# Moving the high and low activation parts of a split-precision trunk to fixed places modulo 512 bytes

## The chip, the cores and the metric

The kernel runs on one core of one Trainium2 chip. What counts is the device time of one launch in microseconds, from the first to the last instruction with a little around them. A time is a median over runs. A profile comes from one execution of its own.

The five engines have short names in the rows below: PE is TensorE (PEld its loading of weights), DVE is VectorE, ACT is ScalarE, POOL is GpSimd, and SP is the queue that issues the DMAs (SPq). SBUF is the on-chip memory, 128 partitions; an address here is always the byte address inside a partition.

## The reference

A decoder trunk of two layers on 256 tokens of width 1024, all in float32:

```python
h = half_step_swiglu(h, ...)            # FFN0:  h + 0.5 * ((silu(hn @ w_gate) * (hn @ w_up)) @ w_down)
h = h + hybrid_dsa_shortconv_mixer(...) # sparse attention next to a short gated convolution,
                                        # one input projection (2472 columns), one output projection
h = half_step_swiglu(h, ...)            # FFN1
h = half_step_swiglu(h, ...)            # FFN2
h = h + conformer_conv_module(...)      # pointwise + GLU, causal convolution of 31 taps, LayerNorm, pointwise
h = half_step_swiglu(h, ...)            # FFN3
return rms_norm(h, final_norm)
```

Each block normalises its input first (`hn` is the RMS norm of `h` times a gain). The inner width of the feed-forward blocks is 2816.

## The kernel before

**Split operands.** Each float32 operand of a projection is held as two parts: a high part, written by ScalarE in the type fp32r that TensorE reads, and a low part, the rest, written by VectorE. A product is three matmuls into the same PSUM tile, which the helper `mm3` issues (lines 254 to 256): weights high with activations high, weights high with activations low, weights low with activations high. In the trace these are `acc<-xh,whi`, `acc<-xl,whi` and `acc<-xh,wlo` (in the trace's names the moving operand comes first). The moving operand is 128 partitions by 256 tokens, 1,024 bytes in a partition; the weights are 128x128. `mm3a` (lines 259 to 261) does it with the activations as the loaded operand, for the first columns of the hybrid layer's input projection.

**Weights.** The class `Stream` brings all weights in tiles of up to 128x2048: a DMA on SP into `raw` (3 buffers), a copy on ScalarE into `whi` (5 buffers), a subtraction on VectorE into `wlo` (5 buffers). It runs ahead of TensorE by some tiles; the next load is issued when `wlo` has been formed. In the built program all of these tiles begin at 256 modulo 512.

**Activations.** `x` is the residual. `xh` and `xl` are its parts times the norm's gain, one tile for each that all blocks share, written by `x_split` (lines 276 to 281) as soon as a slice of `x` is final. Each tile is 128 floats longer than it has to be, and the table `X_AT` says for each norm at which float the part starts in it. In the feed-forward blocks `hh` and `hl` are the parts of the gated product, with places from the table `H_AT`. A feed-forward block has 11 groups of 256 gate and 256 up columns, 8 slices of the contraction each (gate and up), and then 8 output slices of 22 contraction slices (down). In the first group it stops at two places for the norm: `col_stats` (line 306, four matmuls of one column each, `tp<-ones,sqsum`) sums the squares, GpSimd raises the sum to a power (`rc`, line 313), and `row_of` (line 319, four small matmuls, `tp<-con,rc`) spreads the result over the tokens. All other matmuls of a block follow each other without another instruction of TensorE between them.

**Places before**, worked out from the tables and the built program, in bytes modulo 512, high and low:

| block | gate and up, or input projection | down, or output projection |
|---|---|---|
| FFN0 | 192, 192 | 192, 192 |
| hybrid layer | 192, 192 | convolution half (`yh`, `yl`) 192, 192; attention half (`cu`, `q4`) 160, 192 |
| FFN1 | 192, 448 | 192, 448 |
| FFN2 | 192, 64 | 192, 320 |
| conformer | 192, 192 | 128, 256 |
| FFN3 | 192, 320 | 192, 64 |

**The hybrid layer** takes its tiles from the pool `hyb`. `cu` holds the convolution's input (258 columns for each of 4 slices) and is later taken again for the high part of the attention's output; `q4` holds the transposed queries and is taken again for its low part (lines 703 and 704). `pv_out` and `o_lo` write these parts, `wo_part` (line 806) multiplies with them, first `yh` and `yl`, then the attention's. The order of its work is set by a planner, the class `Side`, from costs written out by hand.

Of the kernel before, what the change touches and what calls it, by code (L numbers as in the profile page):

```python
# [10 lines left out]
FT = mybir.dt.float32  # L11
FR = mybir.dt.float32r
# [6 lines left out]
S = 256  # L19
KT = 8  # L20
# [10 lines left out]
RAW_BUFS = 3  # L31
AHEAD = 3

X_AT = ((16, 16), (16, 16), (16, 80), (16, 112), (16, 16), (16, 48))
H_AT = ((112, 112), (112, 48), (112, 16), (112, 80))
DVE_CT = 2
LO_H = (2, 2, 1, 1, 1, 1, 1, 0)

# [150 lines left out]
def trunk_kernel(ctx: ExitStack, tc: tile.TileContext, xT, wgu, wdn, wza, wzq, wcv, wout, wp1, wp2,  # L189
# [33 lines left out]

    x = keep.tile([128, KT, S], FT, name="x")
    x_all = [keep.tile([128, KT * S + 128], FR, name=n) for n in ("xh", "xl")]
    xparts = [[t[:, o:o + KT * S].rearrange("p (k t) -> p k t", k=KT) for t, o in zip(x_all, at)] for at in X_AT]
    par = keep.tile([128, NP], FT, name="par")
    con = keep.tile([128, NC_], FT, name="con")
    ones = keep.tile([128, 128], FT, name="ones")
# [16 lines left out]
    def acc():  # L246
        return psum.tile([128, 512], FT, name="acc", bufs=6)
# [22 lines left out]
    norm = {}  # L270
# [3 lines left out]
        norm["parts"] = []  # L274

    def x_split(d):
        xh, xl = xparts[norm["g"]]
        g = par[:, P_G + norm["g"] * 8 + d:P_G + norm["g"] * 8 + d + 1]
        nc.scalar.activation(xh[:, d], x[:, d], AF.Copy, scale=g)  # L279
        nc.vector.scalar_tensor_tensor(xl[:, d], x[:, d], g, xh[:, d].bitcast(FT),  # L280
                                       op0=OP.mult, op1=OP.subtract)
# [14 lines left out]
    def x_ready(d):  # L296
        x_split(d)
        x_square(d)
# [29 lines left out]

    def ffn(f, gnext, last=False):
        with tc.tile_pool(name=f"ffn{f}", bufs=1, reuse_waits="tile") as fp:  # L330
            xh, xl = xparts[norm["g"]]
            hh, hl = [fp.tile([128, NF * S + 128], FR, name=n)[:, o:o + NF * S].rearrange("p (k t) -> p k t", k=NF)
                      for n, o in zip(("hh", "hl"), H_AT[f])]
            gates = {}

            def gate_out(u, G):
# [85 lines left out]
            for d in range(8):  # L422
                ps = acc()
                for h in range(2):
                    wh, wl = [t[:, :1408].rearrange("p (k c) -> p k c", k=11) for t in st.peek(0)]
                    for k in range(11):
                        kk = h * 11 + k
                        mm3(ps[:, :S], wh[:, k], wl[:, k], hh[:, kk], hl[:, kk], kk == 0, kk == NF - 1)
                    if h == 1:
                        nc.vector.scalar_tensor_tensor(x[:, d], ps[:, :S], 0.5, x[:, d],  # L430
                                                       op0=OP.mult, op1=OP.add)
                        if not last:
                            x_split(d)
                            x_square(d)
                        else:
                            x_square(d)
                            g = par[:, P_G + gnext * 8 + d:P_G + gnext * 8 + d + 1]
                            if d < KT - 1:
                                nc.scalar.activation(x[:, d], x[:, d], AF.Copy, scale=g)
                            else:  # L440
                                nc.vector.tensor_scalar(x[:, d], x[:, d], g, None, op0=OP.mult)
                    st.done()


    def hybrid(gnext):
        with tc.tile_pool(name="hyb", bufs=1, reuse_waits="tile") as hp:
            xh, xl = xparts[norm["g"]]
            z = [hp.tile([128, 936], FT, name=f"z{b}") for b in range(2)]
            zP = [acc() for b in range(2)]
            rc = rstd = None  # L450
# [118 lines left out]
                nc.vector.scalar_tensor_tensor(mk[b], sc[b][:, :NK[b]], -2e38, ncm, op0=OP.is_gt, op1=OP.max)  # L569


            cu = hp.tile([128, 4, S + 2], FT, name="cu")
            nc.gpsimd.memset(cu[:, :, :2], 0.0)
            yh = hp.tile([128, 4, S], FR, name="yh")
            yl = hp.tile([128, 4, S], FR, name="yl")
            cv = hp.tile([128, 4, S], FT, name="cv")

            def proj():
                ps = acc()
                wh, wl = [t.rearrange("p (k c) -> p k c", k=KT) for t in st.peek(0)]  # L580
                for c in range(2):
                    cs = slice(c * 128, (c + 1) * 128)
                    for k in range(8):
                        mm3(ps[:, c * S:(c + 1) * S], wh[:, k, cs], wl[:, k, cs], xh[:, k], xl[:, k], k == 0, k == 7)
                    side.did_pe(2.6)
                    if c == 0:
                        side.fill()
                side.fill()
                st.pop()
                return ps  # L590
# [13 lines left out]
                nc.gpsimd.tensor_tensor(cv[:, o], cv[:, o], bc2(rstd), op=OP.mult)  # L604


            qT2 = hp.tile([128, 2, 4, 128], FT, name="q4")
            qT = [qT2[:, b] for b in range(2)]
            kT = hp.tile([128, S], FT, name="kT")
            kd = [hp.tile([128, 2, 64], FT, name=f"kd{b}") for b in range(2)]  # L610
# [56 lines left out]
            att, pts, oT, rows = [], {}, {}, {}  # L667
# [32 lines left out]

            def pv_out(b):
                if not att:
                    att.append(hp.tile([128, 4, S], FR, name="cu"))
                    att.append(hp.tile([128, 4, S], FR, name="q4"))
                oh, ol = att
                bs = slice(b * 128, (b + 1) * 128)
                nc.vector.tensor_tensor(rows[b], oT[b], rows[b], op=OP.mult)
                on = rows[b].rearrange("p (k t) -> p k t", k=4)
                nc.scalar.activation(oh[:, :, bs], on, AF.Copy)
                rows[b] = on  # L710
# [58 lines left out]
            side.add(0, lambda: [pt_out(1, kb, 1, nc.scalar) for kb in range(2)])  # L769
            side.add_pe(1.8, lambda: pv(1), lat=0.1)  # L770
            side.add(0.6, lambda: pv_out(1))
            side.add_pe(0.9, lambda: ([p_T(0, 0, e) for e in range(2)], [pt_out(0, 0, e, nc.scalar) for e in range(2)]))
            side.add_pe(1.1, lambda: den_rows(0))
            side.add_pe(0.9, lambda: pv(0), lat=0.1)
            side.add(0.6, lambda: o_lo(1))
            side.add(0.6, lambda: pv_out(0))
            side.add(0.6, lambda: o_lo(0))
            side.add(2.2, lambda: (st.hi_to(wo_base + 5), st.lo_to(wo_base + 4)))

            for i in range(2):  # L780
                o = slice(2 * i, 2 * i + 2)
# [14 lines left out]
            for i in range(2):  # L796
                o = slice(2 * i, 2 * i + 2)
                g = proj()
# [44 lines left out]
    def conformer(gnext):  # L843
        with tc.tile_pool(name="conf", bufs=1, reuse_waits="tile") as cp, \
                tc.tile_pool(name="bounce", bufs=1, space=bass.MemoryType.DRAM) as dp:
            xh, xl = xparts[norm["g"]]
            LP = S + TAPS
            LU = S + 28
            u = cp.tile([128, 8, LP], FT, name="u")
# [81 lines left out]
            for i in range(4):  # L931
# [3 lines left out]
                for j, ps in ((0, G), (1, A)):  # L935
# [40 lines left out]
                    n = st.nlo  # L976
# [44 lines left out]
            p, p2 = acc(), acc()  # L1021
# [16 lines left out]
            yh = cp.tile([128, 8, S], FR, name="u4", bufs=2)  # L1038
            yl = cp.tile([128, 8, S], FR, name="u4", bufs=2)
# [58 lines left out]
    for h in range(4):  # L1098
        st.start_hi(0, h)
        st.start_lo(0, h)  # L1100
        for k in (2 * h, 2 * h + 1):
            x_split(k)
    for i in (1, 2):
        for j in range(2):
            st.start_hi(i, j)
            st.start_lo(i, j)
    ffn(0, 1)
    hybrid(2)
    ffn(1, 3)
    ffn(2, 4)  # L1110
    conformer(5)
    ffn(3, 6, last=True)


    o = [[acc() for h in range(2)] for b in range(2)]
# [119 lines left out]
```

## Time and profile before

| | us |
|---|---|
| median of three runs | 967.46 |
| lowest, highest run | 965.59, 969.96 |
| profiled execution | 967.26 |
| its span, first to last instruction | 965.49 |
| TensorE busy in it | 942.3 |
| VectorE, ScalarE, GpSimd busy | 620.5, 442.0, 120.2 |
| granted TensorE clock, mean | 0.995 |

The blocks stand in the span, by TensorE's work, at about: FFN0 6 to 200 us, hybrid layer to 295, FFN1 to 477, FFN2 to 664, conformer to 769, FFN3 to 957. A busy share of 98% says that TensorE hardly ever stands still; it doesn't say how fast matmuls follow each other, since the records of neighbours overlap (a matmul's record lasts 0.28 us where the next begins some 0.11 us after it). For that one counts the matmuls in a stretch of known length.

### The profile page before, as it was taken

The numbers are of one execution on the slowest core, as the hardware profiler recorded it, in microseconds if no ns is written. First come the engines' busy times: TensorE is split into PE (matmuls) and PEld (weight loads), VectorE is DVE, ScalarE is ACT, GpSimd is POOL, SyncE is SP. The second block draws the span as 40 slices with busy tenths as digits, with TensorE's granted clock in tenths as the row PEclk, the third lists the DMA queues.
The fourth block names the chain that finished last, engine by engine and source line by source line (L and its number), as shares of the span: only waits on it lengthen the run. The fifth ranks groups of instructions, "written<-read, shape, count | busy, mean of one in ns | idle before, by whom it ended". The sixth has DMA issues, their size and how long they took to land.

```text
span 965.5 us, 18452 instructions
## 1 busy us (share of the span) xinstructions
PE 942.3 (98%) x8130; PEld 922.5 (96%) x8130; DVE 620.5 (64%) x684; ACT 442.0 (46%) x498; POOL 120.2 (12%) x91
## 2 busy tenths in 40 slices
PE   6999999999999999999999999999997999999997
PEld 5999999999989999999999999999975999999997
DVE  6766655578777766656666655556878776665541
ACT  5554334455565644344544443445442464443441
POOL 3100000231302000002310000024042110000011
PEclk9999999999999999999999999999998999999999
DMA  8564436662255655355755554566562465553541
GB/s 303 226 242 175 148 125 202 218 254 89 88 182 180 248 183 212 122 181 180 268 186 201 176 171 140 179 208 241 175 193 57 164 222 185 193 184 126 189 137 44
DMA packets 32176, 173.68 MB, mean 180 GB/s; under 512 B 3552, under 2 KB 7392, under 8 KB 18144
## 3 DMA queue, kind: packets, MB, share of 16 engines
q1 hardware_dynamic: 32096, 172.51, 51.6%
q8 instruction: 63, 1.03, 0.4%
q14 instruction: 17, 0.14, 0.0%
HBM read 170.56 MB, written 1.93 MB: 179 GB/s over the span
## 4 chain that ended last, share of the span: by engine, by line
PE 91%; DVE 3%; DMA 2%; issue 1%; ACT 1%; POOL 1%; SPq 0%; POOLq 0%; DVEq 0%; ACTq 0%
PE acc L255 28%; PE acc L254 28%; PE acc L256 28%; PE acc L883 1%; DMA u<-ud 1%; DVE wlo L122 1%; POOL rc L313 1%; DMA raw<-in_wgu_dram 1%; PE acc L259 1%; PE acc L261 1%; PE acc L260 1%; ACT xh L279 1%; DVE xl L280 0%; PE tp L319 0%; DVE x L822 0%
## 5 line engine op out<-in xcount | busy, mean ns | idle before, releaser
L254 PE MATMUL acc<-xh,whi 128*128 128x256 f32 x1632 | 458.6, 281 | 6.3 <-ACT xh L279 6.3
L255 PE MATMUL acc<-xl,whi 128*128 128x256 f32 x1632 | 458.9, 281 | 2.8 <-DVE xl L280 2.6
L256 PE MATMUL acc<-xh,wlo 128*128 128x256 f32 x1632 | 456.6, 280 | 0.0
L122 DVE TENSOR_TENSOR wlo<-raw,whi 128x2048 fp32r<-128x2048 f32 (+2 forms) x175 | 364.7, 2098 | 11.6 <-ACT whi L111 11.2
L111 ACT ACTIVATE whi<-raw 128x2048 fp32r<-128x2048 f32 (+2 forms) x175 | 299.2, 1712 | 158.0 <-PE acc L255 102.8
L254 PEld LDWEIGHTS acc<-xh,whi 128*128 128x128 f32 x1632 | 307.6, 188 | 7.5 <-ACT xh L279 6.3
L255 PEld LDWEIGHTS acc<-xl,whi 128*128 128x128 f32 x1632 | 309.0, 189 | 4.6 <-DVE xl L280 4.5
L256 PEld LDWEIGHTS acc<-xh,wlo 128*128 128x128 f32 x1632 | 309.0, 189 | 0.0
L255 PE MATMUL acc<-hl,whi 128*128 128x256 f32 x704 | 197.4, 280 | 0.0
L256 PE MATMUL acc<-hh,wlo 128*128 128x256 f32 x704 | 196.6, 279 | 0.0
L254 PE MATMUL acc<-hh,whi 128*128 128x256 f32 x704 | 196.4, 279 | 0.0
L255 PEld LDWEIGHTS acc<-hl,whi 128*128 128x128 f32 x704 | 132.9, 189 | 0.0
L256 PEld LDWEIGHTS acc<-hh,wlo 128*128 128x128 f32 x704 | 132.9, 189 | 0.0
L254 PEld LDWEIGHTS acc<-hh,whi 128*128 128x128 f32 x704 | 132.0, 188 | 0.0
L339 ACT ACTIVATE gs<-gs 128x512 f32<-128x512 f32 x44 | 27.9, 633 | 148.4 <-DVE gs L338 148.4
L345 DVE TENSOR_TENSOR us<-acc,rstd 128x512 f32<-128x512 f32 x44 | 30.3, 690 | 101.1 <-PE acc L256 101.1
L293 POOL TENSOR_TENSOR sqsum<-sq 128x256 f32<-128x256 f32 x6 | 5.2, 874 | 561.5 <-ACT sq L285 561.5
L293 POOL TENSOR_TENSOR sqsum<-sqsum,sq 128x256 f32<-128x256 f32 x35 | 54.5, 1559 | 149.4 <-ACT sq L285 149.0
L430 DVE SCALAR_TENSOR_TENSOR x<-acc,x 128x256 f32<-128x256 f32 x32 | 13.6, 424 | 87.1 <-PE acc L256 87.1
L338 DVE TENSOR_TENSOR gs<-acc,rstd 128x512 f32<-128x512 f32 x44 | 30.4, 691 | 52.5 <-PE acc L256 45.7
L279 ACT ACTIVATE xh<-x,par 128x256 fp32r<-128x256 f32 x48 | 23.8, 504 | 77.7 <-DVE x L430 65.7
L280 DVE SCALAR_TENSOR_TENSOR xl<-x,par,xh 128x256 fp32r<-128x256 f32 x48 | 28.6, 602 | 18.7 <-ACT xh L279 18.7
(187 smaller groups left out, 685.6 us busy)
## 6 DMA issues: line engine op xcount, KB each, us to landing
raw<-in_wgu_dram SPq DMA_DIRECT2D x85, 1024.0 KB, 4.8
raw<-in_wdn_dram SPq DMA_DIRECT2D x64, 704.0 KB, 4.1
raw<-in_wp_dram SPq DMA_DIRECT2D x12, 1024.0 KB, 4.9
raw<-in_wcv_dram SPq DMA_DIRECT2D x6, 1024.0 KB, 4.8
raw<-in_wout_dram SPq DMA_DIRECT2D x4, 1024.0 KB, 4.8
u<-ud SPq DMA_DIRECT2D x8, 284.0 KB, 4.9
raw<-in_wgu_dram SPq DMA_DIRECT2D x4, 512.0 KB, 8.3
raw<-in_wzq_dram SPq DMA_DIRECT2D x2, 1024.0 KB, 6.3
```

Source lines behind the costliest of these rows:

```text
L111: self.nc.scalar.activation(hi[:, :n], self.raw[i][:, :n], AF.Copy)
L122: self.nc.vector.tensor_tensor(lo[:, :n], raw[:, :n], hi[:, :n].bitcast(FT), op=OP.subtract)
L254: nc.tensor.matmul(ps, wh, ah, start=start, stop=False, skip_group_check=skip)
L255: nc.tensor.matmul(ps, wh, al, start=False, stop=False, skip_group_check=skip)
L256: nc.tensor.matmul(ps, wl, ah, start=False, stop=stop, skip_group_check=skip)
L279: nc.scalar.activation(xh[:, d], x[:, d], AF.Copy, scale=g)
L280: nc.vector.scalar_tensor_tensor(xl[:, d], x[:, d], g, xh[:, d].bitcast(FT), op0=OP.mult, op1=OP.subtract)
L293: nc.gpsimd.tensor_tensor(total, parts[0], sq, op=OP.add)
L338: nc.vector.tensor_tensor(gs, two(G), bc2(rstd), op=OP.mult)
L339: nc.scalar.activation(gs, gs, AF.Silu)
L345: nc.vector.tensor_tensor(us, two(U), bc2(rstd), op=OP.mult)
L430: nc.vector.scalar_tensor_tensor(x[:, d], ps[:, :S], 0.5, x[:, d], op0=OP.mult, op1=OP.add)
```

## The change

Every high part now starts at 192 and every low part at 448 modulo 512. The tables become one pair for `xh` and `xl` and one for all others, used for every block; `xparts[norm["g"]]` gives way to the one pair `xh`, `xl`. In the hybrid layer a helper `pair` makes `yh` and `yl`, and later the attention's two parts, as tiles of 1,152 floats with the same places; `cu` and `q4` get that size too, so that their room can be taken again, and all four are made at the head of the layer. By this the other tiles of that layer move in SBUF. The conformer's output projection keeps its places (128, 256).

The instructions of every engine, their shapes and their order are the same as before. One instruction has one more wait: the small memset of `cu` on GpSimd (line 573) now waits for TensorE too.

```diff
-X_AT = ((16, 16), (16, 16), (16, 80), (16, 112), (16, 16), (16, 48))
-H_AT = ((112, 112), (112, 48), (112, 16), (112, 80))
+X_AT = (16, 80)
+H_AT = (112, 48)
...
-    xparts = [[t[:, o:o + KT * S].rearrange("p (k t) -> p k t", k=KT) for t, o in zip(x_all, at)] for at in X_AT]
+    xh, xl = [t[:, o:o + KT * S].rearrange("p (k t) -> p k t", k=KT) for t, o in zip(x_all, X_AT)]
...
             hh, hl = [fp.tile([128, NF * S + 128], FR, name=n)[:, o:o + NF * S].rearrange("p (k t) -> p k t", k=NF)
-                      for n, o in zip(("hh", "hl"), H_AT[f])]
+                      for n, o in zip(("hh", "hl"), H_AT)]
...
-            xh, xl = xparts[norm["g"]]
+            def pair(names):
+                return [hp.tile([128, 1152], FR, name=n)[:, o:o + 4 * S].rearrange("p (k t) -> p k t", k=4)
+                        for n, o in zip(names, H_AT)]
+
+            yh, yl = pair(("yh", "yl"))
+            cu = hp.tile([128, 1152], FT, name="cu")[:, :4 * (S + 2)].rearrange("p (k t) -> p k t", k=4)
+            qT2 = hp.tile([128, 1152], FT, name="q4")[:, :4 * S].rearrange("p (b a t) -> p b a t", b=2, a=4)
...
-            cu = hp.tile([128, 4, S + 2], FT, name="cu")
             nc.gpsimd.memset(cu[:, :, :2], 0.0)
-            yh = hp.tile([128, 4, S], FR, name="yh")
-            yl = hp.tile([128, 4, S], FR, name="yl")
...
-            qT2 = hp.tile([128, 2, 4, 128], FT, name="q4")
...
                 if not att:
-                    att.append(hp.tile([128, 4, S], FR, name="cu"))
-                    att.append(hp.tile([128, 4, S], FR, name="q4"))
+                    att.extend(pair(("cu", "q4")))
```

## Rows read from the trace of the kernel before

**Rows 1.** The page: busy time by engine, and the chain that ended last.

```profile
PE 942.3 (98%) x8130; PEld 922.5 (96%) x8130; DVE 620.5 (64%) x684; ACT 442.0 (46%) x498; POOL 120.2 (12%) x91
...
PE 91%; DVE 3%; DMA 2%; issue 1%; ACT 1%; POOL 1%; SPq 0%; POOLq 0%; DVEq 0%; ACTq 0%
PE acc L255 28%; PE acc L254 28%; PE acc L256 28%; PE acc L883 1%; DMA u<-ud 1%; DVE wlo L122 1%; POOL rc L313 1%; DMA raw<-in_wgu_dram 1%; PE acc L259 1%; PE acc L261 1%; PE acc L260 1%; ACT xh L279 1%; DVE xl L280 0%; PE tp L319 0%; DVE x L822 0%
```

**Rows 2.** Waits of TensorE and of SP's queue: us in total, times, longest.

```profile
PE acc L254 <- ACT xh L279: 6.3, 1, 6.3
...
SPq L76 <- DVE wlo L122: 776.9, 169, 22.1
```

**Rows 3.** Windows, TensorE: stretch, sum, busy (matmuls), clock, DMA share, GB/s; FFN0 to FFN3.

```profile
30.00:130.00 100.00, 100.00 (x852) 1.00 0.54 193
150.00:200.00 50.00, 50.00 (x427) 1.00 0.62 209
...
320.00:400.00 80.00, 80.00 (x708) 1.00 0.54 190
424.00:474.00 50.00, 50.00 (x443) 1.00 0.65 222
500.00:600.00 100.00, 100.00 (x851) 1.00 0.49 167
610.00:660.00 50.00, 50.00 (x427) 1.00 0.64 216
...
800.00:890.00 90.00, 90.00 (x766) 1.00 0.50 176
905.00:955.00 50.00, 50.00 (x427) 1.00 0.37 121
```

**Rows 4.** The same view: hybrid layer (three stretches), FFN1's first group, conformer (two).

```profile
250.00:254.00 4.00, 4.00 (x36) 1.00 0.01 2
...
256.80:260.80 4.00, 4.00 (x38) 1.00 0.57 231
...
283.80:294.80 11.00, 11.00 (x96) 1.00 0.53 192
306.40:310.20 3.80, 3.80 (x34) 1.00 0.37 121
...
664.20:669.20 5.00, 5.00 (x45) 1.00 0.59 231
675.00:697.00 22.00, 22.00 (x196) 1.00 0.53 178
```

**Rows 5.** Timeline, TensorE, border of FFN1 and FFN2: start us, us, instruction.

```profile
475.96 0.28 PE L255 MATMUL acc<-hl,whi 128*128 128x256 f32 x1
...
476.87 0.28 PE L254 MATMUL acc<-xh,whi 128*128 128x256 f32 x1
476.98 0.28 PE L255 MATMUL acc<-xl,whi 128*128 128x256 f32 x1
...
477.69 0.28 PE L255 MATMUL acc<-xl,whi 128*128 128x256 f32 x1
```

**Rows 6.** Timeline: the matmul behind the small ones (FFN0; FFN1 twice; FFN2; conformer).

```profile
28.26 0.36 PE L254 MATMUL acc<-xh,whi 128*128 128x256 f32 x1
...
306.16 0.36 PE L254 MATMUL acc<-xh,whi 128*128 128x256 f32 x1
...
310.85 0.37 PE L254 MATMUL acc<-xh,whi 128*128 128x256 f32 x1
...
491.80 0.37 PE L254 MATMUL acc<-xh,whi 128*128 128x256 f32 x1
...
674.05 0.37 PE L254 MATMUL acc<-xh,whi 128*128 128x256 f32 x1
```

**Rows 7.** Timeline, GpSimd, head of the hybrid layer.

```profile
210.94 0.10 POOL L573 MEMSET cu<- 128x8 f32 x1
221.69 0.48 POOL L474 TENSOR_TENSOR raa<-z,con 128x144 f32<-128x144 f32 x1 [10.66 <-ACT z L732]
```

More of the change, by code (lines that the diff above doesn't have):

```diff
@@ L330, in ffn @@
         with tc.tile_pool(name=f"ffn{f}", bufs=1, reuse_waits="tile") as fp:
-            xh, xl = xparts[norm["g"]]
             hh, hl = [fp.tile([128, NF * S + 128], FR, name=n)[:, o:o + NF * S].rearrange("p (k t) -> p k t", k=NF)
-                      for n, o in zip(("hh", "hl"), H_AT[f])]
+                      for n, o in zip(("hh", "hl"), H_AT)]
             gates = {}
@@ L446, in hybrid @@
         with tc.tile_pool(name="hyb", bufs=1, reuse_waits="tile") as hp:
-            xh, xl = xparts[norm["g"]]
+            def pair(names):
[4 more added lines that the diff above has]
+            qT2 = hp.tile([128, 1152], FT, name="q4")[:, :4 * S].rearrange("p (b a t) -> p b a t", b=2, a=4)
             z = [hp.tile([128, 936], FT, name=f"z{b}") for b in range(2)]
@@ L845, in conformer @@
                 tc.tile_pool(name="bounce", bufs=1, space=bass.MemoryType.DRAM) as dp:
-            xh, xl = xparts[norm["g"]]
             LP = S + TAPS
```

## The prediction

> **What bounds the kernel now.** I read the page first: TensorE is busy 98% of the span and carries 91% of the chain of work that ended last, nearly all of it in the three matmuls of the helper `mm3` (lines 254 to 256) [rows 1]. Its waits for other engines are small: the largest in sum is 6.3 us, while the queue that loads weights waits 776.9 us for buffers that VectorE frees [rows 2]. So the weight stream is ahead of TensorE nearly everywhere, and the time is the number of matmuls times the distance from one start to the next.
>
> That distance is the second thing to read. The view of windows counts the matmuls that touch a stretch; some two of them began before it, so I take 2 off. Feed-forward 0 (FFN0): 100 us / 850 = 117.6 ns in gate and up, 50 / 425 = 117.6 in down. FFN1: 80 / 706 = 113.3 and 50 / 441 = 113.4. FFN2: 117.8 and 117.6. FFN3: 117.8 and 117.6 [rows 3]. All eight stretches hold the same shape (128x128 weights, 256 columns) at a granted clock of 1.00, and none has a wait in it. So there are two paces, some 113.4 and 117.75 ns, 4.4 ns apart. FFN1 is the only one whose low parts lie at 448 modulo 512 in both halves; FFN0 has 192, FFN2 64 and 320, FFN3 320 and 64.
>
> The third reading says that the address is not all. In the conformer, at 192 and 192 throughout, the stretch from 664.2 runs at 5.0 / 43 = 116 ns and the one from 675 at 22 / 194 = 113.4; in the hybrid layer's projections, at 192 and 192, 4 us hold 38 matmuls in one place and 36 in another; and within FFN1, at 192 and 448, the stretch from 306.4 holds 34 in 3.8 us, 119 ns [rows 4]. So at (192, 192) and at (192, 448) both paces occur, and a stream keeps the one with which it restarted. At (192, 64) and (192, 320) I find the slow one alone. FFN2 shows it at its border, where no other instruction lies between: the eight steps up to its first high part take 476.87 - 475.96 = 0.91 us, 114 ns each, the six steps from its first low part at 64 take 0.71 us, 118 ns each [rows 5].
>
> What sets the pace at a restart shows after the four small transposes of `row_of` (line 319). The matmul behind them takes 0.37 us in FFN1, FFN2, FFN3 and the conformer, and 0.36 in FFN0; the same 0.36 stands behind the column sums in FFN1 (306.16), and the slow stretch of 34 matmuls follows it [rows 6] (FFN3, at 784.40, reads as FFN2 does). Of the four restarts at 0.37, those with low parts at 448 (FFN1) or 192 (conformer) run fast, those at 64 and 320 slow. The 0.36 of FFN0 is followed by slow matmuls to the end of its down projection. That first matmul reads a high part, which doesn't move.
>
> **The change, part by part.** No instruction is added, taken away or reordered; the addresses move. Beside them one memset on GpSimd, that of `cu`, gets a wait for TensorE, because its tile now lies where FFN0's activations were. These are read for the last time before the hybrid layer begins at some 200 us; the memset stands at 210.94 and the next GpSimd work starts at 221.69, after 10.66 us of idle [rows 7]. Queued behind it is the rotary work that waits for ScalarE anyway. I price this wait at nothing, at most its own 0.1 us.
>
> FFN2: 1,056 matmuls of gate and up and 528 of down (11 groups x 2 weights x 2 column halves x 8 x 3, and 8 x 22 x 3). It would arrive fast from FFN1 and stay so at (192, 448); behind the column sums I leave the 36 matmuls slow that are slow in FFN1; behind `row_of` its restart has the 0.37 of FFN1 already. 1,548 x 4.4 ns = 6.8 us.
>
> FFN3: the same, less a dozen matmuls around a wait at its start: 1,536 x 4.4 = 6.8 us.
>
> FFN0: from `row_of` to the end of down are 1,461 matmuls without a break (933 of gate and up, 528 of down), 6.4 us if they turn fast and nothing if they don't. At (192, 192) the fast pace was open to it too, as the conformer shows, and its restart fell on 0.36. The restart behind FFN1's column sums has 0.36 at (192, 448) and is slow. I take nothing, with 6.4 us as the other end.
>
> Hybrid layer: the second half of the output projection (96 matmuls at 160 and 192) holds 96 in 11.0 us, 11.0 / 94 = 117 ns [rows 4]: at 113.4 it gives 0.4 us. Its first half and the six projections are of the kind that has both paces: 0, between +0.5 and -0.9 us (some 100 matmuls fast and 200 slow now).
>
> Conformer: its first 48 matmuls would come in fast from FFN2, 0.2 us. The 216 that are fast now could fall slow, +0.9 us; I take them as they are. Its output projection is not touched.
>
> FFN1 keeps its addresses; I take it as it is. ScalarE and VectorE write the same tiles at other offsets; the loads of weights don't change; the cover at the faster pace is FFN1 itself, where the stream keeps up at 113.4.
>
> Sum: 6.8 + 6.8 + 0.4 + 0.2 = 14.2 us. The profiled execution took 967.26 us (span 965.49), so 953.1; the median of the runs, 967.46, stands 0.2 above it. I say **953.0 us**.
>
> **A rule against it.** The rows show one shape at two paces under one granted clock. The Trainium skill ("TensorE: Matmul & The Clock Gate", section "Step-by-step: what each phase is for") says that TensorE has two independent read ports to SBUF, one for the moving operand and one for weights, so that a weight load takes nothing from the running matmul. By that rule where an operand lies could not matter, and the time would stay. The border of FFN2 [rows 5] speaks against it; it is rival D.
>
> **The rivals.** A is the forecast: FFN2 and FFN3 turn fast, FFN0 stays slow: 953.
>
> B: FFN0 turns fast too. For it: both FFN1 and the conformer run fast behind `row_of`, and the restart in FFN0 and in the conformer comes after a wait for GpSimd's `rc`, whose end need not fall alike in each run. Against it: the 0.36, and that no run of the kernel before came near 961, as one with a fast FFN0 would. 953.0 - 6.4 = 946.6; with the slow projections of the hybrid layer fast as well 945.7.
>
> C: only one of FFN2 and FFN3 restarts fast (or one falls back at the column sums): 953.0 + 6.8 = 959.8.
>
> D: no change. The pace hangs on the state at a restart alone, FFN2 and FFN3 stay as they are, and only the small terms move: 966 to 968.
>
> E, slower: FFN1 loses its pace. Now it enters from slow matmuls at (160, 192); then it would enter from others, and the restart behind its `row_of` could fall on 0.36. It decides at that one matmul. 933 + 528 matmuls at 4.4 ns are 6.4 us, and its first 84 another 0.4; if FFN2 and FFN3 share that restart, nothing is gained there: 967.3 + 6.8 - 0.4 = 973.7.
>
> **How the numbers follow.** A 0.52, B 0.28, C 0.07, D 0.06, E 0.07. The likeliest gives 953.0. The range holds A, B and C (0.87, two in ten would be left out without C and a little of A's edges): the lower end is B's 945.7 less 1.2 us, the upper end C's 959.8 plus 0.7; the runs before spread by -1.9 and +2.5 us around their median, which inside the range needs no more room. So 944.5 to 960.5. About 0.5% (4.8 us) is what a measurement of this kernel can tell from no change: A, B and C lie below 962.6, D within, E above: faster 0.87, same 0.06, slower 0.07.
>
> **What would show it.** In windows of FFN2 and FFN3 some 885 matmuls in 100 us in place of 851, and 443 in 50 of down. At FFN2's start the steps stay at 0.11 to 0.12 us and six of them take 0.68. In FFN0 the matmul behind `row_of` reads 0.36 and 852 stay in the window (A) or 0.37 and some 885 (B). The second half of the hybrid's output projection takes 10.9 us, not 11.3. It would be wrong if FFN2 or FFN3 still counted 851 at (192, 448): then the address was not the cause; or if FFN1 counted 680 in 80 us (E).

## The result: 953.9 us, and the profile after

The changed kernel took 953.86 us (median of four runs, 949.95 to 958.75), the kernel before 966.53 beside it (964.31 to 969.96). The ratio is 0.9879, with a 95% interval of 0.9837 to 0.9921: faster, clear of the noise though under 2%, and 0.9 us above the forecast of 953.0. The same kernel, run again later for six runs, stood at 0.9825 (0.9787 to 0.9863), 948.95 us. So 953.0 lies among this kernel's runs, above the median of the later ones. A ratio leaves out each run that lies more than 1.5% above the fastest of its kernel, here one of the later six and in e1 two of four, though such a run can be the kernel's own at its slower pace. The profile shows where the time went.

First the page of the profile after: busy time of TensorE and its weight loads, then the shares of the chain of work that ended last.

```profile
PE 926.1 (97%) x8130; PEld 905.2 (95%) x8130; DVE 620.7 (65%) x684; ACT 442.8 (47%) x498; POOL 118.8 (13%) x91
...
PE 90%; DVE 4%; DMA 2%; issue 1%; ACT 1%; POOL 1%; SPq 0%; POOLq 0%; DVEq 0%; ACTq 0%
```

The count of matmuls is the same 8,130, TensorE still carries nine tenths of the chain, and it is busy 16.2 us less than before. Nothing was removed, so the matmuls follow each other faster. The view of windows shows where (stretch in us, sum, TensorE's busy time with the matmuls that touch the stretch, granted clock, DMA share, GB/s): gate and up, then down, of FFN0, FFN1, FFN2 and FFN3, with the second half of the hybrid layer's output projection behind FFN0.

```profile
35.00:135.00 100.00, 100.00 (x884) 1.00 0.55 195
145.00:195.00 50.00, 50.00 (x444) 1.00 0.63 215
281.00:291.00 10.00, 10.00 (x90) 1.00 0.57 211
310.00:410.00 100.00, 100.00 (x884) 1.00 0.55 195
420.00:470.00 50.00, 50.00 (x444) 1.00 0.67 228
490.00:590.00 100.00, 100.00 (x885) 1.00 0.53 185
600.00:650.00 50.00, 50.00 (x444) 1.00 0.67 229
...
780.00:880.00 100.00, 100.00 (x885) 1.00 0.52 184
885.00:935.00 50.00, 50.00 (x443) 1.00 0.44 146
```

All four feed-forward blocks now run at FFN1's pace of [rows 3]: 100 us hold 884 or 885 matmuls where FFN2 held 851, 50 us hold 443 or 444 where it held 427. With 2 taken off as before, that is 100 / 882 = 113.4 ns. The clock is 1.00 in every row, as it was. The hybrid projection holds 90 in 10 us, 113.6 ns, where [rows 4] had 117.

The border of FFN1 and FFN2 in the timeline (start us, us, instruction), to be laid beside [rows 5]:

```profile
473.94 0.28 PE L255 MATMUL acc<-xl,whi 128*128 128x256 f32 x1
...
474.62 0.28 PE L255 MATMUL acc<-xl,whi 128*128 128x256 f32 x1
```

Six steps from the first low part take 0.68 us where they took 0.71. In the same place, with the same instructions, the break in the pace is gone.

**Where the span went**, 965.49 to 949.8 us, block by block between the same instructions of the two traces:

| stretch | before, us | after, us | difference |
|---|---|---|---|
| first matmul to FFN0's restart behind `row_of` | 21.9 | 25.1 | +3.2 |
| FFN0, from there | 172.5 | 166.0 | -6.5 |
| hybrid layer | | | -0.4 |
| FFN1 | 181.7 | 182.1 | +0.5 |
| FFN2 | 187.45 | 180.58 | -6.9 |
| conformer | 104.8 | 105.85 | +1.0 |
| FFN3 | 187.8 | 181.0 | -6.8 |

They sum to -15.9 against -15.7 of the span; the other 0.2 is the start of the first matmul, at 6.54 us in place of 6.33. The first row is a matter of that execution: in the second profile of the same kernel (after_again, below) the restart stands where it stood before. These are the four small transposes of `row_of` ahead of it, first in the profile after:

```profile
31.20 0.71 PE L318 MATMUL tp<-con,rc 128*128 128x128 f32 x4 [0.19 <-POOL rc L312]
31.67 0.37 PE L254 MATMUL acc<-xh,whi 128*128 128x256 f32 x1
```

and in the second profile:

```profile
27.81 0.71 PE L318 MATMUL tp<-con,rc 128*128 128x128 f32 x4
28.28 0.37 PE L254 MATMUL acc<-xh,whi 128*128 128x256 f32 x1
```

The 0.37 is the mark that the prediction set for rival B, and FFN0 is at the fast pace, as the window from 35 us shows.

### The profile page after: what moved, and what is told of

Read it like the earlier page. It is cut to its first block, busy times and chain, and to the rows that moved or that the text cites. A ratio compares the mean times of both kernels' runs of the same rounds, so it can differ in the third digit from the quotient of the medians.

```text
span 949.8 us, 18452 instructions
## 1 busy us (share of the span) xinstructions
PE 926.1 (97%) x8130; PEld 905.2 (95%) x8130; DVE 620.7 (65%) x684; ACT 442.8 (47%) x498; POOL 118.8 (13%) x91
## 4 chain that ended last, share of the span: by engine, by line
PE 90%; DVE 4%; DMA 2%; issue 1%; ACT 1%; POOL 1%; SPq 0%; POOLq 0%; DVEq 0%; ACTq 0%
PE acc L255 28%; PE acc L254 28%; PE acc L256 28%; PE acc L881 1%; DVE v L924 1%; DVE wlo L122 1%; POOL rc L312 1%; DMA raw<-in_wgu_dram 1%; DMA u<-ud 1%; PE acc L259 1%; PE acc L261 1%; PE acc L260 1%; ACT xh L278 1%; DVE xl L279 1%; PE tp L318 0%
## 5 line engine op out<-in xcount | busy, mean ns | idle before, releaser
L256 PE MATMUL acc<-hh,wlo 128*128 128x256 f32 x704 | 194.3, 276 | 0.0
L254 PE MATMUL acc<-hh,whi 128*128 128x256 f32 x704 | 194.3, 276 | 0.0
L255 PE MATMUL acc<-hl,whi 128*128 128x256 f32 x704 | 194.3, 276 | 0.0
```

Of the source, the lines that this page charges most:

```text
L254: nc.tensor.matmul(ps, wh, ah, start=start, stop=False, skip_group_check=skip)
L255: nc.tensor.matmul(ps, wh, al, start=False, stop=False, skip_group_check=skip)
L256: nc.tensor.matmul(ps, wl, ah, start=False, stop=stop, skip_group_check=skip)
```

## The experiments

All of them compute everything that the kernel before computes; only places, or the order of a few instructions, differ. Paces below are worked out as in the prediction: the length of a window over its count less 2. One matmul more or less in the count moves such a pace by 0.14 ns in 100 us and by 0.28 in 50.

**e1: is 448 better than 192 for the low parts?** The forecast treats the two as equal.

```diff
-X_AT = (16, 80)
-H_AT = (112, 48)
+X_AT = (16, 16)
+H_AT = (112, 112)
```

> The changed kernel with every low part at 192 in place of 448, high parts at 192 as before. Theory 1 (the fast pace needs the low part at the high part's place or 256 bytes from it; which of the two it is doesn't matter): FFN1, FFN2 and FFN3 run at 113.4 ns, some 885 matmuls in 100 us and 443 in 50 us of down, the hybrid layer's projections show the same fast and slow stretches as before and after, and the time lies with the changed kernel's, 948 to 960 us, the spread being FFN0's. Theory 2 (448 itself, half of 512 away from the high part, is what helps): FFN1 to FFN3 at 117.75 ns, 851 in 100 us, 967.3 + 6.8 - 0.4 = 974 us.

Measured: 958.59 us (962.28, 974.76, 947.28, 954.9), ratio 0.9867 (0.9774 to 0.9961). Gate and up of FFN0, FFN1, FFN2 and FFN3 in the execution of 962.28 us:

```profile
35.00:135.00 100.00, 100.00 (x851) 1.00 0.54 192
...
315.00:415.00 100.00, 100.00 (x885) 1.00 0.55 194
495.00:595.00 100.00, 100.00 (x885) 1.00 0.53 185
785.00:885.00 100.00, 100.00 (x851) 1.00 0.51 178
```

FFN1 and FFN2 are fast at (192, 192), so 448 for the low part is not what makes them so. FFN0 and FFN3 are slow here: they are the blocks that can go either way, and this was the first sign that FFN3 is one of them. The run of 974.76 us lies above the forecast's 960 and where e2 lies below, in which no stretch is fast; it has no trace, so what was slow in it stays open.

**e2: all low parts at 64, in gate and up, in down and in the hybrid layer.** The undoing of the change's core, in every block at once.

```diff
-X_AT = (16, 80)
-H_AT = (112, 48)
+X_AT = (16, 112)
+H_AT = (112, 80)
```

> The changed kernel with every low part at 64 in place of 448, in the hybrid layer's output projection too. Both theories that rest on the address: no stream can be fast, 851 matmuls in 100 us in all four feed-forward blocks and no stretch at 113.4 ns in the conformer, where FFN2's border in the kernel before showed a fast stream falling slow: 967.3 + 6.8 (FFN1) + 1.3 (conformer and hybrid layer) = 975 us. If the restart alone decided and the address did not, FFN1, FFN2 and FFN3 with their 0.37 us restarts would stay fast and the time would be some 953 us.

Measured: 976.97 us, ratio 1.0136 (1.0075 to 1.0197). Gate and up of FFN0 and FFN1, then the conformer:

```profile
35.00:135.00 100.00, 100.00 (x852) 1.00 0.55 195
320.00:420.00 100.00, 100.00 (x851) 1.00 0.50 175
...
684.00:706.00 22.00, 22.00 (x189) 1.00 0.55 173
```

FFN1 falls to 851 and the conformer from 196 in 22 us [rows 4] to 189. The high part stayed where it was, so the place of the low part alone took the fast pace away. The four runs lie within 2.2 us of each other (975.61 to 977.81), those of the changed kernel 8.8 us apart: where no stretch is fast, most of the spread is gone. That fits a spread which is itself a change of pace from run to run.

**e3 and e5: other places, a pair for each block.** One kernel tries seven pairs, since each half of a block can have its own.

```diff
-X_AT = ((16, 16), (16, 16), (16, 80), (16, 112), (16, 16), (16, 48))
-H_AT = ((112, 112), (112, 48), (112, 16), (112, 80))
+X_AT = ((16, 80), (16, 16), (112, 112), (96, 96), (16, 16), (16, 72))
+H_AT = ((112, 48), (80, 16), (64, 0), (112, 56))
```

> The kernel before with other places for each block, high and low: FFN0 192, 448; FFN1 gate and up 64, 64, down 64, 320; FFN2 gate and up 0, 0, down 0, 256; FFN3 gate and up 192, 416, down 192, 480; hybrid layer and conformer 192, 192. Theory 1a (only the distance of high and low counts, 0 modulo 256): FFN1 and FFN2 fast in both halves (885 in 100 us, 443 in 50), FFN3 slow in both (851, 427): some 958 us or, with a fast FFN0, 953. Theory 1b (the place against the weights counts too, which begin at 256: 192 and 448 are good places, others not): FFN1 to FFN3 all at 851 and 427, some 974 us.

Measured: 975.17 us. FFN1's gate and up at (64, 64), FFN2's at (0, 0) and its down at (0, 256):

```profile
315.00:415.00 100.00, 100.00 (x852) 1.00 0.50 176
...
500.00:600.00 100.00, 100.00 (x835) 1.00 0.47 168
615.00:665.00 50.00, 50.00 (x419) 1.00 0.63 217
```

The last two show a third pace: 100 / 833 = 120.0 ns. e5 then asks whether places near 192 do as well, with both parts at the same place:

```diff
-X_AT = ((16, 16), (16, 16), (16, 80), (16, 112), (16, 16), (16, 48))
-H_AT = ((112, 112), (112, 48), (112, 16), (112, 80))
+X_AT = ((16, 80), (16, 16), (8, 8), (24, 24), (16, 16), (20, 20))
+H_AT = ((88, 88), (108, 108), (124, 124), (96, 96))
```

> The kernel before with other places, high and low alike, to see how near to 192 modulo 256 a part has to lie: FFN0 gate and up 192, 448, down 96, 96; FFN1 gate and up 160, 160, down 176, 176; FFN2 gate and up 224, 224, down 240, 240; FFN3 gate and up 208, 208, down 128, 128; hybrid layer and conformer 192, 192. Theory 1b (192 modulo 256 alone is good, against weights at 256): 117.75 to 120 ns in all of these, 851 in 100 us or fewer, the downs no faster. Theory 1c (any place that is the same for both parts modulo 128 or keeps some distance from the weights is good): some of 160, 176, 208, 224, 240 run at 113.4 ns, 885 in 100 us.

Measured: 972.7 us. FFN0's gate and up at (192, 448); FFN0's down at (96, 96); gate and up of FFN1 at (160, 160), of FFN2 at (224, 224) and of FFN3 at (208, 208):

```profile
32.00:132.00 100.00, 100.00 (x885) 1.00 0.56 195
140.00:190.00 50.00, 50.00 (x419) 1.00 0.62 207
310.00:410.00 100.00, 100.00 (x845) 1.00 0.54 190
...
500.00:600.00 100.00, 100.00 (x847) 1.00 0.50 174
...
795.00:895.00 100.00, 100.00 (x859) 1.00 0.51 180
```

The two kernels together:

| high, low modulo 512 | ns a matmul |
|---|---|
| (192, 448) | 113.3 to 113.4 |
| (208, 208) | 116.7 |
| (240, 240) | 117.1 |
| (64, 64), (64, 320), (192, 416) | 117.6 to 117.8 |
| (224, 224) | 118.3 |
| (160, 160), (128, 128), (192, 480) | 118.5 to 118.8 |
| (176, 176) | 119.0 |
| (96, 96), (0, 0), (0, 256) | 119.9 to 120.0 |

Sixteen bytes beside 192, at (176, 176) and (208, 208), the fast pace was not seen; of all pairs tried none but those of 192 and 448 reached it. Each of the other pairs stood in one stretch of one execution.

**e9: the place in memory, or the place relative to the weights?** The weights' tiles begin at 256 in all kernels so far. A pad of 64 bytes ahead of them moves them to 320; the activations' tiles of the trunk stay at (192, 448), while `hh`, `hl` and the hybrid layer's pairs move along with the weights, to (256, 0).

```diff
     ones2 = keep.tile([128, 128], FT, name="ones2")
+    pad = keep.tile([128, 16], FT, name="pad")
+    nc.gpsimd.memset(pad, 0.0)
```

> The changed kernel with 64 bytes put ahead of the weights' tiles: these begin at 320 in place of 256 modulo 512. xh and xl stay at 192 and 448; hh, hl and the hybrid layer's output operands move along with the weights, to 256 and 0. Theory 1b as a distance (a part must lie 64 bytes below the weights modulo 256): gate and up slow in FFN1 to FFN3 and the conformer (851 in 100 us or fewer), the downs fast (443 in 50 us) though they lie at 256 and 0. Theory 1b as a place (192 modulo 256 is good wherever the weights are): gate and up fast, downs at 120 ns as 0 and 256 were in the run with other pairs.

Measured: 975.57 us. Gate and up, then down, of FFN1; FFN3's down (FFN0 and FFN2 read as FFN1 does, and FFN3's gate and up too):

```profile
315.00:415.00 100.00, 100.00 (x845) 1.00 0.53 188
430.00:480.00 50.00, 50.00 (x444) 1.00 0.66 227
...
905.00:955.00 50.00, 50.00 (x427) 1.00 0.45 146
```

What stayed at (192, 448) fell to 845 matmuls, 118.6 ns; what went to (256, 0) runs at 444 in 50 us, a place at which e3's (0, 256) held 419. FFN3's down, also at (256, 0), holds 427: the slow pace is open at the right distance too. So no place is fast by itself. The fast pace is open where both parts lie 64 bytes below the weights, modulo 256; level with the weights, e3 took 120.0 ns. A slow pace follows the distance too: the 118.6 of this gate and up, 128 bytes below the weights, is within a count of the 118.5 of (128, 128) in e5, which lies as far below its own.

ScalarE and VectorE write the weights' tiles, which moved with them here, so their writing could be what the moving operand meets. A stretch of e3's FFN2, at (0, 0), in which VectorE, ScalarE and GpSimd stand still speaks against it (window with TensorE, its loads and these three engines, then two starts in it, 24 matmuls apart):

```profile
593.54:596.53 2.99, 2.99 (x28) 2.99 (x26) 0.00 (x0) 0.00 (x0) 0.00 (x0) 1.00 0.70 234
...
593.53 0.28 PE L254 MATMUL acc<-xh,whi 128*128 128x256 f32 x1
...
596.41 0.28 PE L254 MATMUL acc<-xh,whi 128*128 128x256 f32 x1
```

That is 2.88 us / 24 = 120.0 ns, as in the whole block. Which reads or writes meet inside the chip no run here shows.

**after_again, e4 and e6: why two blocks change from run to run.** FFN0 and FFN3 each restart once behind a wait: FFN0 for `rc`, FFN3 at its head for the last slice of `xh`. (FFN1 waits at its head too, 0.24 and 0.32 us in the profile after, and was fast in every trace at these places, so a wait alone does not settle it.) e4 takes FFN0's wait away: `row_of` comes eight triples later, when `rc` has long been there.

```diff
-                    if u == 1 and j == 0:
+                    if f and u == 1 and j == 0:
                         rstd = row_of(rc)
                     run(0, 1, 0, 8, False)
+                    if not f and u == 1 and j == 0:
+                        rstd = row_of(rc)
```

> The changed kernel with row_of moved in FFN0 alone, behind the second column half of its group 1 in place of between the two, some 2.7 us later, so that TensorE no longer waits for GpSimd's power there. If the wait for another engine is what makes FFN0's pace a matter of chance: the restart then always reads 0.37 us and FFN0 runs at 113.4 ns in the profile and in the timed runs, whose upper half goes: median some 950 us, no run above 955, and 0.4 us of waiting saved besides. If chance lies elsewhere (the loads at the start, the clock): the runs spread from 950 to 959 as those of the changed kernel do.

Measured: 954.84 us (956.72, 954.19, 955.48, 947.76), ratio 0.9893 (0.9829 to 0.9957). Gate and up of FFN0 and FFN3:

```profile
35.00:135.00 100.00, 100.00 (x885) 1.00 0.56 195
...
780.00:880.00 100.00, 100.00 (x852) 1.00 0.50 180
```

FFN0 is fast in this execution; one run still lies 6.4 to 9 us below the others, so a chance is left, FFN0's or FFN3's. FFN3 is slow, at the very places at which it was fast in the profile after. e6 takes FFN3's wait away instead: the first group does four slices of the contraction for all four output tiles and then the other four, so that the last slice of `xh` is wanted later.

```diff
-                for k0, k1 in ((0, 6), (6, 8)):
+                for k0, k1 in ((0, 4), (4, 8)):
                     for j in range(2):
...
-                            if k1 == 8 and (j, c) == (0, 1):
+                            if k1 == 8 and (j, c) == (1, 0):
                                 rc = norm_cols()
```

> The changed kernel with the first group of FFN1, FFN2 and FFN3 in contraction slices 0 to 3 and then 4 to 7, in place of 0 to 5 and 6 and 7, so that TensorE doesn't wait for late slices of xh and xl at the head of the block (some 1.1 us in FFN1, 0.4 in FFN3); the column sums stay behind as many matmuls as before. Theory a (a wait for another engine in the stream, in FFN0 behind row_of and in FFN3 at its head, is what makes the pace there a matter of chance): FFN3 is fast in the profile and in every run, the runs fall into two clusters some 6.5 us apart by FFN0 alone, near 950 and 956. Theory b (chance lies elsewhere): FFN3 is slow in some runs still and the runs spread over 13 us.

Measured: 952.79 us (947.59, 952.68, 954.3, 952.9, 945.91, 953.83), ratio 0.9849 (0.981 to 0.9887). FFN0 and FFN3:

```profile
32.00:132.00 100.00, 100.00 (x885) 1.00 0.55 195
775.00:875.00 100.00, 100.00 (x884) 1.00 0.52 184
```

The runs fall into two groups, 945.9 to 947.6 and 952.7 to 954.3, some 6.5 us apart: what one block is worth. That fits one chance left, FFN0's, with FFN3 fast throughout. It doesn't prove the wait to be FFN3's whole cause, since only one of the six runs has a trace.

The changed kernel, unchanged, ran beside e6:

> The changed kernel itself once more, for the spread of its runs. Theory a: FFN0 and FFN3 each fast or slow by chance, FFN1 and FFN2 always fast: runs at some 947 to 952 (both fast), 953 to 958 (one), 960 to 964 (none). The profile shows 885 in 100 us in FFN1 and FFN2. If FFN1 or FFN2 were left to chance too, some runs would lie above 966.

Measured: 948.95 us (946.83, 949.11, 948.03, 955.4, 948.79, 962.56), ratio 0.9825 (0.9787 to 0.9863). The 962.56 lies where the expectation put a run with neither FFN0 nor FFN3 fast; it has no trace. Gate and up of the four blocks in the execution of 946.83 us:

```profile
32.00:132.00 100.00, 100.00 (x885) 1.00 0.55 195
305.00:405.00 100.00, 100.00 (x884) 1.00 0.57 197
490.00:590.00 100.00, 100.00 (x885) 1.00 0.51 176
775.00:875.00 100.00, 100.00 (x885) 1.00 0.53 184
```

All four are fast and nothing is late at the start: 946.83 us beside 946.6 that rival B gave.

**e7: all three together.** e4's and e6's edits, and the conformer's output projection moved from (128, 256) to (192, 448):

```diff
-            yh = cp.tile([128, 8, S], FR, name="u4", bufs=2)
-            yl = cp.tile([128, 8, S], FR, name="u4", bufs=2)
+            yh, yl = [cp.tile([128, 8 * LU], FR, name="u4", bufs=2)[:, o:o + 8 * S].rearrange("p (k t) -> p k t", k=8)
+                      for o in (16, 48)]
```

> The kernel with the split of slices 0 to 3 and 4 to 7, with FFN0's row_of behind the second column half as in the run with the late row, and with the conformer's output projection at 192 and 448 in place of 128 and 256. Theory a: no block is left to chance, all four feed-forward blocks at 113.4 ns (885 in 100 us) in every run, the output projection of the conformer at 113.4 in place of 120 ns (64 times 20 ns, 1.3 us): 951.6 - 1.5 - 1.3 - 0.4 = 948.4 us, all runs within 4 us, the start's loads being what is left. Theory b: runs as far apart as those of the changed kernel, 945 to 958.

Measured: 946.47 us (944.13 to 951.51, six runs), ratio 0.9801 (0.9766 to 0.9835): the lowest median of all, though its interval overlaps that of the changed kernel beside it. The runs lie 7.4 us apart where theory a allowed 4, and the profiled one, of 950.15 us, is among the upper two. The conformer's output projection in the profile after:

```profile
745.00:760.00 15.00, 15.00 (x127) 1.00 0.55 211
```

and in e7, with FFN0's gate and up of that execution first:

```profile
32.00:132.00 100.00, 100.00 (x851) 1.00 0.54 188
...
745.00:765.00 20.00, 20.00 (x179) 1.00 0.57 211
```

120.0 ns became 113.0, 1.3 us over its 192 matmuls. But FFN0 is slow in this trace, and in e4 it was fast, with the same instructions around the same late `row_of` and no wait in either. Something ahead of the restart differs. One thing that does is in the weight loads just before it (line, engine, operation, count, busy us, mean ns), e4:

```profile
L255 PEld LDWEIGHTS acc<-xl,whi 128*128 128x128 f32 x7 | 1.3, 192 | 0.0
...
```

and e7:

```profile
L256 PEld LDWEIGHTS acc<-xh,wlo 128*128 128x128 f32 x7 | 1.3, 192 | 0.0
...
```

In a slow stretch at these places one load of each three takes 192 ns and the other two 188, and which one it is differs: the second of the three in e4, the third in e7. In the traces with both parts at 192 or 448 and the weights at 256, the feed-forward blocks restart 24 times behind `row_of` without a wait. The second load was the long one ahead of 21 of them, and all 21 ended fast; the third was ahead of two (e7's FFN0, e4's FFN3), and both ended slow. The last one (e1's FFN3) arrived at the fast pace and left slow. So the slow pace has several forms, and the form in which a stream arrives goes with how it leaves. In FFN0 that form differs between executions already ahead of the column sums; which event of the start sets it I could not tell. It was read from traces, not brought about by an edit.

**e8: does a longer wait force the fast pace?** From the last matmul's start to the first small one's, FFN0's gap for `rc` was 463 to 467 ns in two traces (after, e3), and FFN0 was fast in both; at 371 to 375 ns it was fast in three (after_again, e5, e6) and slow in two (before, e1). e8 is e7 with FFN0's `row_of` three matmuls ahead of its first place, so that the wait is long.

```diff
-                    run(0, 0, 0, 8, False)
+                    cut = 7 if f == 0 and u == 1 and j == 0 else 8
+                    run(0, 0, 0, cut, False)
                     if u == 1 and j == 0:
                         rstd = row_of(rc)
+                    run(0, 0, cut, 8, False)
```

> The kernel of the run in which everything was to be smooth, but with FFN0's row_of three matmuls before its place in the changed kernel (ahead of slice 7 of the first column half of group 1), so that TensorE waits longer for GpSimd's power, some 730 us-thousandths in place of 371 to 375 ns. Theory c (read from nine traces: a restart behind a wait of 463 ns and more has always been fast, 14 of 14, whatever the stream was before; behind 371 to 375 ns it was fast three times in five): FFN0 is fast in every run, 885 matmuls in 100 us, and the runs lie at 944 to 948 us with no second cluster. Theory d (the length of the wait doesn't matter, the stream's state before it does): the second cluster at 950 to 952 stays, one run in three or so.

Measured: 951.04 us (945.78, 955.72, 951.24, 950.84, 955.6, 947.67), ratio 0.9865 (0.9825 to 0.9905). The runs still lie 10 us apart, where the theory put all of them at 944 to 948. FFN0 is fast in the trace of the lowest run, behind a gap of 803 ns. Which block was slow in the others isn't seen, as they have no trace; so the forecast of the theory fell, and the theory with it unless it was a block other than FFN0.

## Why the prediction was right, and where it wasn't

**The cause held.** The step on which most of it stands, that the pace is a matter of where the operand lies and that FFN2 leaves the slow pace at (192, 448), is right, and right in size: 6.8 us forecast for FFN2, 6.9 measured; 6.8 for FFN3, 6.8 measured; 0.4 for the attention half of the output projection, 11.3 to 10.9 us. e2 undid it and e9 made it sharper: what counts is the distance to the weights. The wait of the memset costs nothing, as priced: in GpSimd's timeline it runs at 207.86, and the work behind it waits another 10.67 us for ScalarE, as in [rows 7].

```profile
207.86 0.10 POOL L576 MEMSET cu<- 128x8 f32 x1
218.63 0.49 POOL L478 TENSOR_TENSOR raa<-z,con 128x144 f32<-128x144 f32 x1 [10.67 <-ACT z L731]
```

**Rival D fell.** One shape under one granted clock runs at 113.4, 117.8 or 120.0 ns: the 120.0 by its place, the other two by its place and by how the stream restarted. The Trainium skill ("TensorE: Matmul & The Clock Gate", section "Step-by-step: what each phase is for") gives TensorE independent read ports for the moving operand and the weights. By it the weights' place could not matter to the running matmul; e9 shows that it does.

**FFN0's term was mis-sized.** "I take nothing, with 6.4 us as the other end": in the profile it gave 6.5, and rival B's mechanism, which had 0.28, is what both profiles of the changed kernel show. The step that failed was the reading of FFN0's restart as slow in each run. (The stretch holds 936 and 528 matmuls, 1,464 and not 1,461; at 4.4 ns that is 6.4 us all the same.) The mark that it read was sound in itself: the matmul behind FFN0's `row_of` takes 0.37 us in both profiles of the changed kernel and in e4 and e6, where FFN0 is fast, and 0.36 in e1 and e7, where it is slow; e1's reads

```profile
30.00 0.36 PE L254 MATMUL acc<-xh,whi 128*128 128x256 f32 x1
```

The error was to take the 0.36 of one execution for a property of the kernel. "No run of the kernel before came near 961" rested on three runs; later runs of it took 960.92, 961.05, 961.43 and 961.55 us. A fast FFN0 in those would explain them, which is argued and not shown, as none of them has a trace. A smaller reading was off too: the 116 ns of the conformer's first stretch comes from a window of 5 us, in which two counts weigh much. From the first to the last start, 664.31 to 669.85 us, the 48 matmuls stand 117.9 ns apart, so at (192, 192) that stretch was slow, and the conclusion that both paces occur there stays.

**FFN3 was taken as sure and isn't.** The prediction gave it FFN2's working. e1 and e4 have it slow at (192, 192) and (192, 448). Of the four blocks only FFN1 and FFN2 came out fast in every trace whose pairs were of 192 and 448 and whose weights lay at 256; e1's untraced run of 974.76 us leaves open whether this holds in every run. So rival C's mechanism occurs, in some executions, and with it the 959.8 that it gave is within reach of the first four runs' 958.75.

**So the median hit for a mixed reason.** The forecast was a kernel with FFN0 slow and FFN3 fast in each run. What exists is a kernel whose two blocks of some 6.5 us each fall either way: about 947 us with both fast, some 953 with one, some 960 with none. That hit was luck in part: the first four runs had a median near the middle one, the later ones nearer the lowest. Nor does a time alone tell how many blocks were fast. In the one profiled execution of the first four, of 951.59 us, both were, and the 6.5 us that FFN0 gave beyond the forecast's sum were partly taken back by the late start (+3.2) and the conformer and FFN1 (+1.0 and +0.5).

**The small terms.** The conformer was to gain 0.2 and lost 1.0, about the +0.9 that the prediction kept as its other end, though not by the way it named: its stretch from 664.5 us still holds 197 matmuls in 22 us. FFN1 lost 0.5 in waits at its head; it kept its pace, so rival E did not come about in any trace at these places. What took the conformer's 1.0 shows in the first batch of its convolution by matmuls, in the timeline of before and then of after:

```profile
700.79 7.11 PE L883 MATMUL acc<-u,w 128*32 128x256 f32 x128 [1.99 <-DMA u<-ud]
```

```profile
690.70 8.80 PE L881 MATMUL acc<-u,w 128*32 128x256 f32 x128 [2.02 <-DMA u<-ud]
```

The windows over the two batches, of before and then of after:

```profile
700.80:708.00 7.20, 7.20 (x129) 1.00 0.68 274
```

```profile
690.70:699.50 8.80, 8.80 (x129) 0.81 0.66 246
```

After a wait of 2.0 us for a DMA in both, the granted clock was 1.00 in one and 0.81 in the other, so part of the batch ran at the lower of TensorE's two levels, 1.2 in place of 2.4 GHz, and 1.7 us went; a later batch gave back a part of it. In the second profile of the changed kernel the first batch waited longer and stayed at the higher level:

```profile
687.60 7.11 PE L881 MATMUL acc<-u,w 128*32 128x256 f32 x128 [2.33 <-DMA u<-ud]
```

There the conformer took 104.5 us (651.00 to 755.49) against 104.8 before, a gain near the 0.2 of the forecast. So the 1.0 is not in every execution of the changed kernel, and the length of the wait doesn't decide it. No edit here was made to bring this about or to prevent it.

## What to carry to other kernels

When TensorE is nearly always busy, count its matmuls in windows of the same length, stage by stage: the busy share read 97 or 98% while the distance between matmuls differed by 4 to 6%, and nearly all of what this change gained lay there. If two stages of one shape differ at one clock, sweep the place of the moving operand against that of the loaded weights, with another pair in each stage so that one kernel tries many. And before a single trace is taken as the kernel, look whether its runs fall into groups: a gap of the size of one stage's gain suggests that the stage changes its pace from run to run, and a trace of a run of each group would show it.

## What the runs showed of the hardware

For matmuls of 128x128 weights and 256 columns in fp32r, issued in threes on two sets of weights with a load ahead of each, the distance between starts was 113.3 ns at best, with both moving parts 64 bytes below the weights modulo 256; 120.0 ns with them level, and at (96, 96) too; and between 116.7 and 119.0 at the other places tried. At the best place two paces were seen, 113.4 and 117.8, and each lasted until the stream was next interrupted or the place changed; a few small matmuls were interruption enough. At the other places no stretch reached the fast pace.
